# Gathering tokens for a pair of experts with the model's dimension along the free axis, and padding the skipped branches of 32 experts

## The chip, the core and the metric

The kernel runs on one core of a Trainium2 chip, in one launch. The core has five engines, each with an instruction stream of its own: PE (matrix products; weight loads are shown as PEld), DVE and ACT (element work), POOL, and SP, which here issues nearly all DMAs. The metric is the device time of one execution in microseconds, here the median of three runs: 1147.12 us (1146.0 to 1147.28).

## The reference

One layer of a trunk for 256 tokens of 1024 numbers, in float32: a block of three mixers (a short convolution and two kinds of attention) and a layer of 32 experts, of which each token uses four. What matters here is the second half:

```python
logits = (xt @ router_w + router_b)
top_vals, top_idx = lax.top_k(logits, TOP_K)              # TOP_K = 4
top_w = jax.nn.softmax(top_vals, axis=-1)
combine = jnp.einsum('tk,tke->et', top_w, jax.nn.one_hot(top_idx, N_EXPERTS))
def expert_step(acc, params):
    w1, b1, w2, b2, gate_e = params
    u = xt @ w1 + b1
    glu = jnp.minimum(u[:, ::2], SWIGLU_LIMIT)
    lin = jnp.clip(u[:, 1::2], -SWIGLU_LIMIT, SWIGLU_LIMIT)
    a = glu * jax.nn.sigmoid(SWIGLU_ALPHA * glu) * (lin + 1)
    out = a @ w2 + b2
    return acc + gate_e[:, None] * out, None
```

`w1` has 1024x2048 and `w2` 1024x1024 numbers for each expert, 12 MB together.

## The kernel before

About the first 183 us are the mixers, the second norm and the router. Then come 32 experts in a fixed order (the loop over `e`, line 1056). Each reads its weights as twelve tiles of 1 MB, `we{e}_0` to `we{e}_11`, over SP's queue. Twenty tiles are held in a ring of buffers of four kinds (`RING`, line 34); a load is issued by `prefetch` (line 849, the DMA is line 858) when the buffer's last reader is done.

An expert works on 64 slots (`CAP`), the first 64 tokens that chose it. Per pair of experts, `Prepare` (line 759) makes a one-hot matrix `oh` of tokens by 2 x 64 slots, and gathers with products of the normed tokens `xn2` and `oh` into `xg`, which stands with the model's dimension on the partitions; `modulated2` (line 740) scales and shifts it by ACT and DVE. This is done in the middle of the odd expert before the pair; the first pair is gathered earlier, with `half` called piecewise at line 828, before the experts begin.

For each expert PE does the up products `u` in two halves (`first`, line 876), turns the result (`aT`), and does the down products `o` (`second`, line 906). DVE weighs `o` (line 1088), and after each second expert `scatter` adds the pair's `y` to the tokens (line 937). Every product and every turn goes through `mm` or `turn`, so PE's rows all bear lines 83 and 86; tiles tell them apart. A product in float32 shows as two MATMUL rows in the trace and two weight loads.

Where an expert has more than 64 tokens, `if_more` (line 1020) runs before the expert's main path: up to four further blocks of slots, each behind a branch on the count (line 1021). With these inputs that happens for experts 5 and 16, each time with the first block alone (32 more slots). For all others PE jumps over about 1600 instructions. The count is read from memory in `tokens` (line 1047), and `hint` (line 803) puts a branch hint at the start of each main path. `behind_branch` (line 1027) keeps the main path's products behind the branch. The order within one engine is made by a scheduler from the order of the code and the dependencies.

Of the kernel before, what the change touches and what calls it, by code (L numbers as in the profile page):

```python
# [18 lines left out]
P = 128  # L19
# [3 lines left out]
NT = S // P  # L23
# [9 lines left out]
KINDS = {"l": 7, "h": 8, "x": 2, "c": 3}  # L33
RING = "lhhllccchlhhhxhhlllx"
CAP = 64
MORE = ((64, 32), (96, 64), (160, 64), (224, 32))


# [5 lines left out]
def bcast(ap, n):  # L44

    return ap.rearrange("p (a o) -> p a o", o=1).to_broadcast([ap.shape[0], ap.shape[1], n])
# [3 lines left out]
def trunk(ctx: ExitStack, tc: tile.TileContext, x_d, p1_d, p2_d, be_d, ada_d, win_d, wout_d, w1_d, w2_d, out_d):  # L50
    nc = tc.nc
# [10 lines left out]
    def t2k(name, dtype=F32):  # L62
        return tmp.tile([P, 512], dtype, tag="t2", name=name)
# [7 lines left out]
    def pa(name):  # L71
        return psA.tile([P, 2, 512], F32, tag="A", name=name)
# [4 lines left out]
    def pb(name):  # L77
        return psB.tile([P, 512], F32, tag="B", name=name)
# [3 lines left out]
    def mm(out, lhsT, rhs, start, stop):  # L82
        last[:] = [nc.tensor.matmul(out, lhsT, rhs, start=start, stop=stop, skip_group_check=True).ins]  # L83

    def turn(out, in_):
        last[:] = [nc.tensor.transpose(out, in_, ident).ins]  # L86
# [37 lines left out]
    ident = const.tile([P, P], F32, name="ident")  # L124
# [36 lines left out]
    SEL6 = SELE[:, 0:6]  # L161
    slots = const.tile([P, CAP + 32], F32, name="slots")
    iote = const.tile([P, NE], F32, name="iote")
# [25 lines left out]
    for name in order.split():  # L189
        kind, c = name[0], int(name[1:])  # L190
# [66 lines left out]
    xn2 = const.tile([P, NT, D], F32, name="xn2")  # L257
# [440 lines left out]
    def gates(t):  # L698

        nc.scalar.activation(ex[t], lg[t], AF.Exp, bias=rs[t][:, 0:1])  # L700
        nc.vector.scalar_tensor_tensor(weight[:, t, :], ex[t], 1.0, mask[t], op0=ALU.mult, op1=ALU.mult,
                                       accum_out=rs[t][:, 1:2])
        nc.vector.reciprocal(rs[t][:, 2:3], rs[t][:, 1:2])
        nc.vector.tensor_scalar(weight[:, t, :], weight[:, t, :], rs[t][:, 2:3], None, op0=ALU.mult)
# [14 lines left out]
    pos = const.tile([P, NT, NE], F32, name="pos")  # L719
# [9 lines left out]
    def onehot(oh, base, m, es, pos):  # L729

        at = slots[:, base:base + m].rearrange("p (o c) -> p o c", o=1).to_broadcast([P, len(es), m])
        nc.vector.tensor_tensor(oh, at, bcast(pos[:, es[0]:es[0] + len(es)], m), op=ALU.is_equal)

    def gather(ps, oh, t, w, ks=range(KD)):

        for k in ks:
            mm(ps[k * w // 512][:, k * w % 512:k * w % 512 + w], xn2[:, t, k * P:(k + 1) * P], oh.rearrange("p e c -> p (e c)"),
               t == 0 and k * w % 512 == 0, t == NT - 1)

    def modulated2(xg, ps, w):  # L740
        for k in (0, 4, 1, 5, 2, 6, 3, 7):
            o = xg[:, k].rearrange("p e c -> p (e c)")
            x = ps[k * w // 512][:, k * w % 512:k * w % 512 + w]
            if k > 3:
                nc.vector.tensor_scalar(o, x, s2[:, k:k + 1], t2[:, k:k + 1],  # L745
                                        op0=ALU.mult, op1=ALU.add)
            else:
                nc.scalar.activation(o, x, AF.Identity, scale=s2[:, k:k + 1], bias=t2[:, k:k + 1])  # L748

    def slots_first(sc, og, name):  # L750

        ps = pb(f"og{name}")
        for t in range(NT):
            turn(ps[:, t * P:(t + 1) * P], og[:, t].rearrange("p e c -> p (e c)"))
        nc.scalar.copy(sc, ps[:, 0:S])
# [3 lines left out]
    class Prepare:  # L759


        def __init__(self, e):
            self.e = e
            self.oh = sm.tile([P, NT, 2, CAP], F32, tag="part", name=f"oh{e}")
            if e:
# [5 lines left out]
        def half(self, t, ks=range(KD)):  # L771
            if 0 in ks:
                onehot(self.oh[:, t], 0, CAP, [self.e, self.e + 1], pos[:, t])
            gather(self.ps, self.oh[:, t], t, 2 * CAP, ks)

        def rest(self):
            e = self.e
            xg = sm.tile([P, KD, 2, CAP], F32, tag="xg", bufs=1, name=f"xg{e}")
            modulated2(xg, self.ps, 2 * CAP)
            og = sm.tile([P, NT, 2, CAP], F32, tag="part", name=f"og{e}")  # L780
            ox = sm.tile([P, NT, 2, 32], F32, tag="ox", name=f"ox{e}")
            sc = sm.tile([P, S], F32, tag="sc", name=f"sc{e}")
            for t in range(NT):
                if e == 0:
                    gates(t)
                onehot(ox[:, t], CAP, 32, [e, e + 1], pos[:, t])
                nc.vector.tensor_tensor(og[:, t], self.oh[:, t], bcast(weight[:, t, e:e + 2], CAP), op=ALU.mult)
            slots_first(sc, og, e)
            pick = sm.tile([P, 2, P], F32, tag="pick", name=f"pick{e}")
            for i in range(2):  # L790
                nc.gpsimd.tensor_copy(pick[:, i].rearrange("p (q m) -> p q m", q=2).bitcast(F32R),
                                      sel2[:, :, e + i:e + i + 1].to_broadcast([P, 2, CAP]))
            rows[e // 2] = pick
            for i in range(2):
                ready[e + i] = xg[:, :, i, :], sc, ox[:, :, i, :]

    def prepare(e):
        p = Prepare(e)
        for t in range(NT):
            p.half(t)  # L800
        p.rest()

    def hint(e):
# [215 lines left out]

    def if_more(n_e, e, a, aT, blocks=MORE):  # L1020
        with tc.If(n_e > blocks[0][0], label=f"few{e}") if blocks is MORE else tc.If(n_e > blocks[0][0]):  # L1021
            more(e, a, aT, *blocks[0])
            if blocks[1:]:
                if_more(n_e, e, a, aT, blocks[1:])

    @contextmanager
    def behind_branch():
# [19 lines left out]
    def tokens(e):  # L1047

        traced = nc.cur_bb.bb.instructions
        n = len(traced)  # L1050
        value = nc.values_load(cnt[0:1, e:e + 1], min_val=0, max_val=S)
        return value, next(i for i in traced[n:] if i.engine == mybir.EngineType.PE)

    late = None
    n_next, _ = tokens(0)
    for e in range(NE):
        if e:
            prefetch(4)
        xg, sc, _ = ready[e]
        aT = [t1k(f"aT{e}_{G}").rearrange("p (j s) -> p j s", j=2) for G in range(2)]  # L1060
        n_e = n_next
        if_more(n_e, e, t1k(f"am{e}", "partp"), t1k(f"aTm{e}"))
        with behind_branch():
            if e + 1 < NE:
# [12 lines left out]
        if e % 2 and e + 1 < NE:  # L1077
            prepare(e + 1)
# [13 lines left out]
    o, sc, _ = late  # L1092
# [72 lines left out]
```

## Time and profile before

| | |
|---|---|
| median of three runs | 1147.12 us (1146.0 to 1147.28) |
| the profiled execution | 1146.89 us |
| its span, first to last instruction | 1144.9 us |
| PE matmul busy | 1069.5 us (93%) |
| DVE, ACT busy | 389.2 us (34%), 178.6 us (16%) |
| read from HBM | 446.63 MB |
| mean DMA rate | 393 GB/s |
| mean granted PE clock | 0.985 |

PE's matmuls are pipelined and their ends are modelled, so 93% is not PE at its peak. Times below are microseconds from the span's start. An engine's name with a q (SPq, PEldq) is that engine's queue or sequencer: what it issues or waits for beside its work. A stretch's line in the table of windows gives each engine's busy time with its count of instructions, then PE's granted clock (1.00 is full), the busy share of the DMA engines and their rate. "A <- B: t, n, m" in the waits says that A waited t us for B in all, n times, m us at most.

### The profile page before, as it was taken

Reading aid. Unit: us, or ns where it says so; the run is one execution under the profiler, and the core shown is the slowest. Engines: PE = TensorE matmul, PEld = TensorE weight load, DVE = VectorE, ACT = ScalarE, POOL = GpSimd, SP = SyncE. Lnnn points to the kernel's source line nnn. Section 1 sums busy time; section 2 is a strip of 40 time slices with the busy share of each in tenths; the row PEclk is TensorE's granted clock in tenths of the full one; section 3 lists DMA queues with packets and bytes.
Section 4 is the critical chain, followed back from the end, with each engine's and each line's share of the span. In section 5 each row is a group of like instructions: output and inputs, shape, how many; then the busy total and the mean of one; then the engine's idle time right before and its main releaser. Section 6 shows DMA issues by size and latency. Waiting matters only on the chain. (4 is left out here: it accounts for less than half of the span.)

```text
span 1144.9 us, 14101 instructions
## 1 busy us (share of the span) xinstructions
PE 1069.5 (93%) x5432; PEld 467.1 (41%) x5432; DVE 389.2 (34%) x879; ACT 178.6 (16%) x412; POOL 14.5 (1%) x52
## 2 busy tenths in 40 slices
PE   2999999999989999999999989999999999898987
PEld 2887844343333333433333433434343434242322
DVE  7799933222232223222222222232232322231222
ACT  3458622010101010101010100101010101010100
POOL 1000000000000000000000000000000000000000
PEclk7899999999999999999999989999999999999999
DMA  9888899999987999999999999999999999999992
GB/s 383 360 297 311 331 409 370 416 418 417 418 353 309 417 418 417 418 418 417 417 418 416 419 399 404 419 418 418 417 417 419 417 418 417 411 416 410 416 413 110
DMA packets 62913, 449.54 MB, mean 393 GB/s; under 512 B 6960, under 2 KB 7472, under 8 KB 8624
## 3 DMA queue, kind: packets, MB, share of 16 engines
q1 hardware_dynamic: 62336, 447.11, 95.6%
q8 instruction: 79, 1.29, 0.5%
q10 hardware_dynamic: 432, 0.59, 0.1%
q14 instruction: 66, 0.54, 0.1%
HBM read 446.63 MB, written 1.05 MB: 391 GB/s over the span
## 5 line engine op out<-in xcount | busy, mean ns | idle before, releaser
L83 PE MATMUL u<-we,xg 128*64 128x512 f32 (+1 forms) x2304 | 494.2, 577 | 12.7 <-DMA we<-in_w 11.3
L83 PEld LDWEIGHTS u<-we,xg 128*64 128x64 f32 (+1 forms) x2304 | 154.0, 134 | 299.9 <-issue 260.4
L83 PE MATMUL o<-we,aT 128*64 128x512 f32 x1024 | 236.5, 598 | 3.7 <-DMA we<-in_w 3.3
L891 DVE TENSOR_SCALAR sw<-u 128x256 f32<-128x256 f32 (+1 forms) x68 | 28.3, 417 | 441.6 <-PE u L83 429.5
L892 ACT ACTIVATE sw<-sw 128x256 f32<-128x256 f32 (+1 forms) x68 | 27.9, 411 | 666.8 <-DVE sw L891 666.8
L83 PEld LDWEIGHTS o<-we,aT 128*64 128x64 f32 x1024 | 69.6, 136 | 133.2 <-issue 121.8
L1088 DVE TENSOR_TENSOR o<-o,g 64x512 f32<-64x512 f32 x64 | 44.1, 689 | 162.2 <-PE o L83 161.7
L83 PE MATMUL y<-o,sc 128*128 128x512 f32 (+1 forms) x160 | 67.1, 592 | 2.1 <-DVE o L1010 1.3
L83 PEld LDWEIGHTS xg<-oh,xn 128*128 128x128 f32 x512 | 58.6, 192 | 12.6 <-issue 12.4
L83 PE MATMUL xg<-oh,xn 128*128 128x128 f32 x512 | 62.1, 279 | 0.1
L236 DVE SCALAR_TENSOR_TENSOR a<-a,silurow 128x1024 f32<-128x1024 f32 x48 | 57.2, 1216 | 0.0
L745 DVE TENSOR_SCALAR xg<-xg,mods 128x128 f32<-128x128 f32 x64 | 26.0, 410 | 62.7 <-ACT xg L748 61.5
L83 PE MATMUL u<-b,pick 128*128 128x512 f32 x64 | 31.0, 484 | 17.3 <-PEq L1021 16.7
L83 PEld LDWEIGHTS y<-o,sc 128*128 128x128 f32 (+1 forms) x160 | 26.5, 197 | 41.8 <-issue 33.4
L944 DVE TENSOR_TENSOR xr<-xr,y 128x1024 f32<-128x1024 f32 x30 | 36.6, 1221 | 11.8 <-PE y L83 10.4
L904 ACT COPY aT<-aT 128x256 f32<-128x256 f32 x64 | 23.8, 372 | 106.1 <-PE aT L86 106.0
L748 ACT ACTIVATE xg<-xg,mods 128x128 f32<-128x128 f32 x64 | 28.9, 457 | 56.4 <-PE xg L83 45.9
L83 PEld LDWEIGHTS u<-b,pick 128*128 128x128 f32 x64 | 12.1, 189 | 57.1 <-issue 55.9
L86 PEld LDWEIGHTS aT<-ident,a 128*128 128x128 f32 x128 | 14.2, 141 | 50.7 <-issue 33.9
L895 DVE TENSOR_TENSOR a<-a,sw 128x256 f32<-128x256 f32 x64 | 27.4, 428 | 6.8 <-ACT sw L892 0.3
L86 PE MATMUL aT<-ident,a 128*128 128x128 f32 x128 | 27.2, 294 | 2.0
L83 PE MATMUL op<-o,yT 128*128 128x512 f32 x64 | 29.0, 600 | 0.0
(299 smaller groups left out, 750.3 us busy)
## 6 DMA issues: line engine op xcount, KB each, us to landing
we<-in_w SPq DMA_DIRECT2D x383, 1024.0 KB, 19.9
a<-in_ada SPq DMA_DIRECT2D x24, 1024.0 KB, 7.0
w<-in_win SPq DMA_DIRECT2D x12, 1024.0 KB, 11.0
o<-in_wout SPq DMA_DIRECT2D x4, 1024.0 KB, 5.8
xr<-in_x SPq DMA_DIRECT2D x1, 1024.0 KB, 5.3
we<-in_w SPq DMA_DIRECT2D x2, 512.0 KB, 18.1
b1in<-in_be SPq DMA_DIRECT2D x1, 512.0 KB, 5.3
out<-xr SPq DMA_DIRECT2D x2, 256.0 KB, 2.0
```

Source lines behind the costliest of these rows:

```text
L83: last[:] = [nc.tensor.matmul(out, lhsT, rhs, start=start, stop=stop, skip_group_check=True).ins]
L86: last[:] = [nc.tensor.transpose(out, in_, ident).ins]
L236: nc.vector.scalar_tensor_tensor(w[:, i], w[:, i], 1.0, silu_row, op0=ALU.mult, op1=ALU.mult, accum_out=mods[:, m, k:k + 1])
L745: nc.vector.tensor_scalar(o, x, s2[:, k:k + 1], t2[:, k:k + 1], op0=ALU.mult, op1=ALU.add)
L748: nc.scalar.activation(o, x, AF.Identity, scale=s2[:, k:k + 1], bias=t2[:, k:k + 1])
L891: nc.vector.tensor_scalar(gl, u[:, 0:n], 7.0, None, op0=ALU.min)
L892: nc.scalar.activation(sg, gl, AF.Sigmoid, scale=1.702)
L895: nc.vector.tensor_mul(ln, ln, sg)
L904: nc.scalar.copy(aT.rearrange("p j s -> p (j s)"), ps[:, 0:n])
L944: nc.vector.tensor_add(xr[:, t, :], xr[:, t, :], y.rearrange("p h m -> p (h m)"))
L1088: nc.vector.tensor_mul(o[64 * (e % 2):64 * (e % 2) + 64, 512 * h:512 * h + 512], ps[r, :], g2[r, :])
```

## The change

`Prepare` gets a second way to gather, `beside`, and `prepare` calls it for all pairs but the first. It multiplies the other way round: the one-hot matrix is the weight and 512 columns of the tokens run through, so that the result `xs` has slots on the partitions and the model's dimension along. Four products replace sixteen. ACT copies the two halves out of PSUM, and eight turns of 128x128 put them into `xg` as before.

In the innermost branch of `if_more` (taken only by an expert with more than 224 tokens) `FILL[e]` turns of the identity are added, whose result nobody reads. They lengthen PE's stream between the branch and the main path.

```diff
+FILL = (99, 1, 93, 100, 107, 116, 107, 115, 107, 116, 107, 115, 107, 116, 107, 115, 107, 116, 107, 115, 107, 116, 107, 115, 107, 116, 107, 115, 107, 116, 107, 0)
...
+        def beside(self):
+
+            at = pa(f"xs{self.e}")
+            for t in range(NT):
+                onehot(self.oh[:, t], 0, CAP, [self.e, self.e + 1], pos[:, t])
+            for h in range(2):
+                for t in range(NT):
+                    mm(at[:, h, :], self.oh[:, t].rearrange("p e c -> p (e c)"), xn2[:, t, h * 512:h * 512 + 512], t == 0, t == NT - 1)
+            for h in range(2):
+                xs = t2k(f"xs{self.e}_{h}")
+                nc.scalar.copy(xs, at[:, h, :])
+                for k in range(4):
+                    turn(self.ps[h][:, k * P:(k + 1) * P], xs[:, k * P:(k + 1) * P])
+
...
     def prepare(e):
         p = Prepare(e)
-        for t in range(NT):
-            p.half(t)
+        p.beside()
         p.rest()
...
             if blocks[1:]:
                 if_more(n_e, e, a, aT, blocks[1:])
+            elif FILL[e]:
+                fill = pb(f"fill{e}")
+                for _ in range(FILL[e]):
+                    turn(fill[:, 0:P], ident)
```

PE in expert 7, where the pair of experts 8 and 9 is gathered, before (u7 and o7 are the up and down products, og8 the gates' turn; a last x4 is four rows alike):

```order
L83 MATMUL u7_1_7393<-we7_7_6064,xg6_6000 64x512 x4
L83 MATMUL xg8_7433<-oh8_7432,xn2_246 128x128 x16
L86 MATMUL og8_7468<-ident_80,og8_7461 128x128 x2
L1051 TENSOR_LOAD cnt_1525
L83 MATMUL o7_7475<-we7_8_6744,aT7_0_6779 64x512 x4
L86 MATMUL aT7_1_7480<-ident_80,a7_1_7412 128x128 x2
```

The same place with the change, where lines 83 and 86 have become 86 and 89:

```order
L86 MATMUL u7_1_8142<-we7_7_6593,xg6_6525 64x512 x4
L86 MATMUL xs8_8183<-xn2_246,oh8_8181 128x512 x4
L89 MATMUL og8_8218<-ident_80,og8_8211 128x128 x2
L1071 TENSOR_LOAD cnt_1525
L86 MATMUL o7_8225<-we7_8_7377,aT7_0_7412 64x512
L89 MATMUL xg8_8182<-ident_80,xs8_0_8190 128x128 x4
L89 MATMUL xg8_8182<-ident_80,xs8_1_8196 128x128 x4
L86 MATMUL o7_8225<-we7_8_7377,aT7_0_7412 64x512 x3
L89 MATMUL aT7_1_8230<-ident_80,a7_1_8161 128x128 x2
```

Four products and eight turns stand for the sixteen products; the gates' turn and one product of `o` have come between the products and the turns.

PE at the start of expert 0's main path, before (y0_224 is the last product of the fourth block that is jumped over, u0_0 the first up products of the path):

```order
L83 MATMUL y0_224_01_2260<-o0_224_2251,sc0_224_2104 128x256 x2
L83 MATMUL y0_224_10_2264<-o0_224_2251,sc0_224_2104 128x256 x2
L83 MATMUL y0_224_11_2268<-o0_224_2251,sc0_224_2104 128x256 x2
L1021 UNCONDITIONAL_BRANCH x5
L1161 BRANCH_PREFETCH_HINT
L83 MATMUL u0_0_2273<-b1_222,pick0_1630 128x512
L83 MATMUL u0_0_2273<-we0_0_1633,xg0_1602 64x512 x4
```

With the change:

```order
L86 MATMUL y0_224_01_2260<-o0_224_2251,sc0_224_2104 128x256 x2
L86 MATMUL y0_224_10_2264<-o0_224_2251,sc0_224_2104 128x256 x2
L86 MATMUL y0_224_11_2268<-o0_224_2251,sc0_224_2104 128x256 x2
L89 MATMUL fill0_2272<-ident_80 128x128 x87
L1037 UNCONDITIONAL_BRANCH x5
L1181 BRANCH_PREFETCH_HINT
L86 MATMUL u0_0_2373<-b1_222,pick0_1630 128x512
L86 MATMUL u0_0_2373<-we0_0_1633,xg0_1602 64x512 x4
```

The path itself is the same. The fill's turns (87 here and 12 among the rows ahead of these, each a weight load and a matmul) have moved it by 198 places, and with it the branch on expert 1's count at the path's end, which the scheduler puts ahead of the last seven products of `o`. In the later experts the paths with a gather also have 32 instructions fewer.

## Rows read from the trace of the kernel before

**Rows 1.** From the page: of the 40 slices (28.6 us each) the DMA engines' busy share and the rate.

```profile
DMA  9888899999987999999999999999999999999992
GB/s 383 360 297 311 331 409 370 416 418 417 418 353 309 417 418 417 418 418 417 417 418 416 419 399 404 419 418 418 417 417 419 417 418 417 411 416 410 416 413 110
```

**Rows 2.** The table of windows: stretch, its length, PE, PEld, DVE, ACT and POOL busy with their counts, PE's granted clock, DMA share, GB/s.

```profile
344.60:348.80 4.20, 4.12 (x11) 1.33 (x13) 1.33 (x7) 0.00 (x0) 0.00 (x0) 0.59 0.01 2
348.80:670.00 321.20, 308.74 (x1569) 118.67 (x1565) 82.65 (x187) 30.91 (x79) 3.19 (x12) 1.00 1.01 415
670.00:700.00 30.00, 28.49 (x116) 10.22 (x116) 9.73 (x18) 1.20 (x3) 0.00 (x0) 0.83 0.97 387
700.00:1108.00 408.00, 388.48 (x1757) 143.68 (x1757) 102.86 (x225) 36.61 (x92) 3.19 (x12) 1.00 1.01 416
...
1122.00:1132.00 10.00, 8.63 (x36) 2.23 (x34) 1.60 (x4) 0.79 (x2) 0.00 (x0) 1.00 0.07 28
```

**Rows 3.** SP's own queue: its longest sum of waits from 323 to 350 us, the issue that ended that wait (start, length), and the longest sum from 660 to 700 us.

```profile
SPq L858 <- PE u L83: 24.2, 1, 24.2
...
348.72 0.33 SPq L858 DMA_DIRECT2D we<-in_w  x1
...
SPq L858 <- PE u L83: 22.8, 9, 8.8
```

**Rows 4.** The chain of work that ended last, in order of time (start, length, what): the links near the end.

```profile
1001.44 20.86 DMA we<-in_w
...
1022.39 19.91 DMA we<-in_w
...
1112.57 19.88 DMA we<-in_w
...
1132.58 3.67 PE o L83 x16
```

**Rows 5.** The table of windows for the first and the fifth of the stretches from one expert's start to the next, and what PE waited for from 348 to 700 us (of weights).

```profile
182.70:210.30 27.60, 27.22 (x112) 9.02 (x112) 5.65 (x19) 4.18 (x9) 1.48 (x2) 1.00 0.97 383
...
296.90:323.00 26.10, 25.97 (x111) 8.88 (x111) 6.67 (x12) 1.58 (x4) 0.00 (x0) 1.00 1.02 418
...
PE o L83 <- DMA we<-in_w: 3.1, 3, 1.3
```

**Rows 6.** PE in order of time (start, length, operation, shapes, count): the eight turns of h2ps and the products behind them; the gather in expert 5 with the next two rows; the scatter in expert 6 with the row behind it.

```profile
162.33 1.04 PE L86 MATMUL h2ps<-ident,xr 128*128 128x128 f32 x8
163.28 1.98 PE L83 MATMUL op<-o,yT 128*128 128x512 f32 x4
...
362.57 3.84 PE L83 MATMUL xg<-oh,xn 128*128 128x128 f32 x32
366.25 0.38 PE L86 MATMUL og<-ident,og 128*128 128x128 f32 x2
366.56 1.94 PE L83 MATMUL o<-we,aT 128*64 128x512 f32 x8
...
381.99 3.70 PE L83 MATMUL y<-o,sc 128*128 128x512 f32 x8
385.52 0.38 PE L86 MATMUL aT<-ident,a 128*128 128x128 f32 x2
```

**Rows 7.** ACT: copies of 128x512 out of PSUM (count, ns least, median, most), and the sigmoid beside the gather of rows 6.

```profile
L661 ACT COPY h2T<-h2ps x2: 585/585/585, 163.0 to 173.2; 128x512 f32<-128x512 f32 x2
...
363.14 0.42 ACT L892 ACTIVATE sw<-sw 128x256 f32<-128x256 f32 x1 [6.24 <-DVE sw L891]
```

**Rows 8.** PE's own branches on the counts (count, ns least, median and most, first and last start us): all of them, and one each behind experts 0, 3, 9, 10, 16 and 29.

```profile
L1021 PEldq COMPARE_BRANCH  x36: 74/348/6017, 181.2 to 1104.2; - x36
...
L1021 PEldq COMPARE_BRANCH  x1: 430/430/430, 204.3 to 204.3; - x1
...
L1021 PEldq COMPARE_BRANCH  x1: 3181/3181/3181, 292.1 to 292.1; - x1
...
L1021 PEldq COMPARE_BRANCH  x1: 6017/6017/6017, 479.4 to 479.4; - x1
...
L1021 PEldq COMPARE_BRANCH  x1: 5092/5092/5092, 507.5 to 507.5; - x1
...
L1021 PEldq COMPARE_BRANCH  x1: 5982/5982/5982, 701.7 to 701.7; - x1
...
L1021 PEldq COMPARE_BRANCH  x1: 3722/3722/3722, 1073.2 to 1073.2; - x1
```

**Rows 9.** PE's first work behind a branch (start, length, what, count, idle time before it and what ended it): behind expert 0, behind expert 5, and behind experts 9 and 10.

```profile
206.78 3.64 PE L83 MATMUL o<-we,aT 128*64 128x512 f32 x14 [0.28 <-PEq L1021]
...
374.57 0.47 PE L83 MATMUL u<-b,pick 128*128 128x512 f32 x1 [0.41 <-PEq L1021]
...
485.82 0.47 PE L83 MATMUL u<-b,pick 128*128 128x512 f32 x1 [1.99 <-PEq L1021]
...
513.05 0.47 PE L83 MATMUL u<-b,pick 128*128 128x512 f32 x1 [1.06 <-PEq L1021]
```

**Rows 10.** PE's first 32 up products of expert 5, behind its extra rows, and of expert 6.

```profile
345.08 8.75 PE L83 MATMUL u<-we,xg 128*64 128x512 f32 x32
...
374.97 7.09 PE L83 MATMUL u<-we,xg 128*64 128x512 f32 x32
```

**Rows 11.** From the page's DMA queues: the larger kind of instruction transfers (count, MB, share of 16 engines).

```profile
q8 instruction: 79, 1.29, 0.5%
```

## The prediction

> **What bounds the kernel now.** I began with the page's slices. From the sixth on the core reads about 417 GB/s nearly throughout, with two dips [rows 1], so the expert stage is a stream of weights and the question is where the stream stops. Windows answer that [rows 2]: between 344.60 and 348.80 us the DMA share is 0.01, from 348.80 to 670 it is 1.01, from 670 to 700 it is 0.97, from 700 to 1108 again 1.01. The waits of SP's own queue say why it stops at 345: one issue, at 348.72, waited 24.2 us for PE's products [rows 3], longer than the 20 us that a load takes from issue to landing at full stream [rows 4], so the queue ran dry. In 660 to 700 the longest wait for PE was 8.8 us [rows 3], and the queue still held work.
>
> The last window is the strangest. From 1122 to 1132 us the share is 0.07 and the rate 28 GB/s [rows 2]: 0.07 of sixteen DMA engines is about one engine. So one engine finishes some 11 us after the others, and the chain of waits hangs on it: links of 19.9 and 20.8 us, each a load from issue to landing, up to 1132.44, then only the last products and the store [rows 4]. A link of eight loads takes about 19.9 us, and most have 0.9 us on top. This engine was given work without a pause from the restart at 348.7 on, so I take the end to be the restart plus a fixed amount. Then only what moves the restart moves the time.
>
> The restart is PE's doing. In the five stretches from 182.70 to 323.00 PE is busy nearly all the time (27.22 of 27.60 us in the first, 25.97 of 26.10 in the last) [rows 5]; it is the clock of that stage, up to the extra rows of expert 5, whose main path begins at 344.7. After 348.8 PE runs against a stream that is slower than itself (from 348 to 700 it waits 3.1 us for weights in all [rows 5]) and its time is slack, as long as SP's waits stay under about 20 us.
>
> **The change part by part.** *The gather.* A pair's gather is now 32 PE rows from 362.57 to 366.25, that is 3.68 us [rows 6]. It becomes four products of 128x512 and eight turns. Four such products in fp32 with a 128x128 weight are the scatter's eight rows, 381.99 to 385.52: 3.53 us. Eight turns of 128x128 took 0.95 us from 162.33 to 163.28 [rows 6]. So a pair costs 3.53 + 0.95 - 3.68 = 0.8 us more. The turns wait for two ACT copies of 128x512, 0.585 us each [rows 7]. The first copy runs under the second pair of products (1.77 us). The second has the two turns of og (366.25 to 366.56, 0.31 us), one product of o and the first four turns over it, together about 1.0 us against 0.585 and a semaphore way of some 0.1 at either end; I cost it at nothing, and at 0.6 us a pair if that cover is gone. ACT is free at that point (its sigmoid ends at 363.56) [rows 7]. The modulation behind the turns gets xg about 1.5 us later, and has some 4 us before the next path begins; hidden. Before the restart two pairs are gathered this way (for experts 2 and 4; that of experts 0 and 1 is unchanged): +1.6 us, between +1.2 and +2.8.
>
> *The placing.* The fill products stand in the innermost branch, which does not run here; they only move addresses. What an address does is seen in the durations of PE's own branches. The median of 36 is 0.35 us, and a few take up to 6.0 [rows 8]. I counted the places in PE's compiled stream, label marks left out, and took each branch's place in a block of 256: 187 took 5.98 us, 188 took 6.02, 203 took 5.09, 204 took 3.18, 220 took 3.72. The four from 235 to 252 took 0.35 to 2.06, those at 1 to 172 at most 0.5. [...] Four microseconds of that are covered, since PE's sequencer runs ahead of its array: a path usually begins with a gap of 0.41 us, and behind two of the three longest waits with 1.99 and 1.06 [rows 9].
>
> Counted so, the new paths do not begin at one place. With label marks in the count they do (place 3 or 4 each time), but there are nine marks for each expert, and the durations above fall in line only without them; then the start falls from 250 (expert 0) by 8 to 10 per expert. So the branches behind experts 6 to 29 come to lie at harmless places or under cover; the losses at 485 and 513 go, but they lie behind the restart and are slack. Before the restart the placing hurts once. The branch behind expert 0, at place 1 before, comes to 198, between 188 and 204. There the cover is thin: it starts at 204.3, and PE's array has work only to 206.5 [rows 8, 9]. A branch of d us lets PE go on at about 204.3 + d + 0.4: with d = 3.18 that is 1.1 us late, with 5.09 it is 3.0, with 6.02 it is 3.9. I take 4.6 (nearer to the neighbour at 203) and so +2.5 us, with 0 and +3.9 as ends. The branch behind expert 3 comes to 214; with 3 to 5 us it stays under its 4.6 us of cover, at worst +0.6. That behind expert 4 (188) falls through, which took 0.08 us before.
>
> *The clock.* [...] Expert 5's first 32 products took 8.75 us instead of 7.09 [rows 10]. As nearly all products before the restart were slow, a shift can only give up to 1.8 us back. I take none.
>
> *Elsewhere.* At 670 to 700 PE would be later against the stream by five more pairs, 4 us, less 2.2 for the two long gaps gone. A wait of 8.8 + 2 us is still under 20, so the last engine does not pause. The tail behind 1132.44 has no changed line.
>
> Sum: +1.6 + 2.5 = +4.1 us. The profiled execution took 1146.89 us (span 1144.9 and 2.0 around it), 0.23 under the median of 1147.12. 1146.89 + 4.1 = **1151.0 us**.
>
> **The rivals.** *Only the gather counts.* The target may come in time behind expert 0: before, place 204 waited 2 us less than place 203, so the place alone does not settle it. Then +1.6: 1148.5.
>
> [...]
>
> *Not slower: the engine that ends last has less to read.* Its 0.9 us on top of a link comes about once for each expert (25 between the restart and the end, 24 us). If these were PE's instruction reads (79 of 16 KB on the page [rows 11], about two for each expert), paths within one block could halve them, -12 us: 1151 - 12 = 1139. Against it: they come once and PE's reads twice. From five fewer of them on the kernel is no longer slower.
>
> *The waits go as named.* If paths did begin on a block, the gaps of 0.28 to 0.41 us before the restart (four) could go, -1.4, against +1.6 for the gather: 1147.1.
>
> *Worse.* The second copy uncovered (+0.6 a pair), the full wait behind expert 0 (+3.9), and 0.6 behind expert 3: 1.6 + 1.2 + 3.9 + 0.6 = +7.3, 1154.
>
> **How the numbers follow.** The forecast (1149.5 to 1152.5) 0.48, only the gather 0.26, waits gone 0.08, worse 0.12, fewer reads 0.06. A measurement of this kernel tells about 0.2%, 2.3 us, from no change, so slower begins at 1149.4: the forecast nearly whole, worse, and a little of the second (0.04) make 0.63; faster is the fewer reads and a lucky clock, 0.07; the rest 0.30 is the same. The range of 8 in 10 leaves out the fewer reads and half of the worse case: 1147.0 to 1153.6.
>
> **What would show it.** The branch near 204 us takes 3 to 6 us, and the 14 products of o behind it begin at 208 to 210 rather than 206.78. Products of xs take 3.5 us and turns 0.95, without a gap between. Expert 5's extra rows and the long wait of SP end about 4 us later, at 352.8 rather than 348.7, and from there to the last landing it is again 783.7 us. A chain with fewer links of 20.8, a DMA share that is 1.01 through 344 to 349, or a landing time that does not follow the restart would prove me wrong.

## The result and the profile after

The changed kernel takes 1160.71 us (median of 5; 1157.70 to 1161.41) against 1147.28 us of the kernel before in the same session: ratio 1.0108, 95% interval 1.0091 to 1.0126. So it is slower, as forecast, but by 13.4 us where 4.1 were forecast, and outside the range of 1147.0 to 1153.6. The profiled execution took 1160.65 us (span 1158.6), 13.76 more than that of before.

The page's slices of the changed kernel (29.0 us each), the DMA engines' busy share and the rate, answer to [rows 1]:

```profile
DMA  9888899999996999999999997999999999999993
GB/s 382 354 304 318 338 390 385 362 406 382 417 392 240 380 418 419 418 418 417 418 418 418 417 403 298 418 417 418 417 419 417 417 417 418 418 418 417 419 417 158
```

The dip at slice 13 is deeper (240 instead of 309), the slice behind it has one too (380), and slice 25 (695 to 724 us) fell to 298; before, the dip there was 399 at its lowest. The windows show the same places in the columns of [rows 2]:

```profile
206.20:210.70 4.50, 0.00 (x0) 0.00 (x0) 0.11 (x1) 0.00 (x0) 0.00 (x0) 1.00 1.01 410
210.70:214.30 3.60, 3.56 (x10) 1.21 (x12) 1.08 (x6) 0.00 (x0) 0.00 (x0) 0.53 0.59 241
...
354.20:358.40 4.20, 4.20 (x13) 1.27 (x15) 1.19 (x6) 0.00 (x0) 0.00 (x0) 0.59 0.01 2
...
400.00:690.00 290.00, 282.24 (x1340) 99.19 (x1336) 75.19 (x173) 31.81 (x78) 2.66 (x10) 1.00 1.01 418
690.00:712.00 22.00, 15.88 (x54) 5.56 (x54) 5.60 (x9) 0.79 (x2) 0.00 (x0) 0.77 0.68 267
712.00:1121.00 409.00, 402.36 (x1668) 138.00 (x1666) 102.67 (x226) 44.44 (x107) 3.19 (x12) 1.00 1.01 416
```

From 206.20 to 210.70 PE does nothing at all, and in the 3.6 us behind that its granted clock is 0.53. The dry queue before expert 5's main path is the same as before, only later. From 690 to 712 the DMA engines are busy for 0.68 of the time: a second dry queue, which before did not have.

PE's own branches behind experts 0 and 5, expert 16's inner one, and the one behind expert 30 (columns as in [rows 8]):

```profile
L1037 PEldq COMPARE_BRANCH  x1: 6732/6732/6732, 203.7 to 203.7; - x1
...
L1037 PEldq COMPARE_BRANCH  x1: 5537/5537/5537, 381.0 to 381.0; - x1
...
L1037 PEldq COMPARE_BRANCH  x1: 5977/5977/5977, 690.2 to 690.2; - x1
...
L1037 PEldq COMPARE_BRANCH  x1: 345/345/345, 1118.1 to 1118.1; - x1
```

Behind expert 0, PE in order of time; then the gather of a pair at 430 us, which answers to [rows 6]:

```profile
203.12 2.79 PE L86 MATMUL o<-we,aT 128*64 128x512 f32 x10
210.74 5.34 PE L86 MATMUL o<-we,aT 128*64 128x512 f32 x14 [4.83 <-PEq L1037]
...
429.80 3.70 PE L86 MATMUL xs<-xn,oh 128*128 128x512 f32 x8
433.33 0.38 PE L89 MATMUL og<-ident,og 128*128 128x128 f32 x2
433.64 1.07 PE L86 MATMUL o<-we,aT 128*64 128x512 f32 x2
434.65 1.09 PE L89 MATMUL xg<-ident,xs 128*128 128x128 f32 x8
435.67 1.93 PE L86 MATMUL o<-we,aT 128*64 128x512 f32 x6
437.54 0.44 PE L89 MATMUL aT<-ident,a 128*128 128x128 f32 x2
```

Against [rows 9] the 14 rows of o start at 210.74 instead of 206.78 and take 5.34 instead of 3.64 us. In the gather the turns stand inside o's products. Eight rows of o took 1.94 us before [rows 6]; here two take 1.07 us by themselves and the other six 1.93 more. An o product is written in two column halves (two rows each). Where the halves stood one behind the other, the trace has two rows under way at once (from 366.60 to 366.90 us before, and again from 435.72 to 436.05 here), and a couple took 0.94 us (eight rows in 1.87, from 366.56 to 368.43). The turns part one such couple; its first half ran with no row beside it (from 433.70 to 434.00) and took 1.01 us, from 433.64 to 434.65, and the six rows behind the turns took as long as eight in a row, 1.87 us from 435.67 to 437.54: 1.0 us lost for each pair of experts.

ACT's copies of the same pair:

```profile
433.59 1.07 ACT L789 COPY xs<-xs 128x512 f32<-128x512 f32 x2 [2.81 <-PE xs L86]
```

Both copies begin behind the last product (PE's next rows, og's turns, begin at 433.33, the copies at 433.59). The first does not run under the second half of the products.

SP's own queue, the longest waits for PE around 358 us, at 380 and from 660 to 730 us (sum, count, longest):

```profile
SPq L874 <- PE u L86: 26.5, 2, 25.2
...
SPq L874 <- PE o L86: 7.3, 1, 7.3
...
SPq L874 <- PE u L86: 32.8, 9, 17.5
```

The first answers to the 24.2 us of [rows 3] and ends at 358.15 instead of 348.72. The last was 8.8 us before. The chain of work that ended last looks as in [rows 4]:

```profile
1125.31 20.86 DMA we<-in_w
...
1146.30 3.67 PE o L86 x16
```

The end is still set by one DMA engine that lags: from 1140 to 1146 us the DMA engines' busy share is 0.06 to 0.08, about one of sixteen. From SP's restart to the last products it is 1146.30 - 358.15 = 788.15 us, before 1132.58 - 348.72 = 783.86. So of 13.7 us, 9.4 arose ahead of the restart and 4.3 behind it. The trace also has the landing of each load. Counted from the restart and set against before, the lagging engine's landings lose 1.6 us up to the 20th load and 2.7 more from 700 to 730 us, and nothing elsewhere.

### The profile page after: what moved, and what is told of

Its sections match the earlier page's. It is cut to its first block, busy times and chain, and to the rows that moved or that the text cites. A ratio compares the mean times of both kernels' runs of the same rounds, so it can differ in the third digit from the quotient of the medians.

```text
span 1158.6 us, 13666 instructions
## 1 busy us (share of the span) xinstructions
PE 1092.1 (94%) x5192; PEld 450.4 (39%) x5192; DVE 389.1 (34%) x879; ACT 194.5 (17%) x442; POOL 14.4 (1%) x52
## 5 line engine op out<-in xcount | busy, mean ns | idle before, releaser
L86 PE MATMUL o<-we,aT 128*64 128x512 f32 x1024 | 253.1, 602 | 6.2 <-PEq L1037 4.8
L86 PEld LDWEIGHTS o<-we,aT 128*64 128x64 f32 x1024 | 72.9, 137 | 138.2 <-issue 135.5
L86 PE MATMUL xs<-xn,oh 128*128 128x512 f32 x120 | 55.5, 605 | 0.0
L86 PEld LDWEIGHTS xs<-xn,oh 128*128 128x128 f32 x120 | 21.6, 190 | 33.7 <-issue 33.7
```

## The experiments

All kernels were compared with the kernel before, run in the same session (medians of 1146.85 to 1147.60 us). The diffs are against the changed kernel, but the last one. Since FILL stands in code that does not run, other numbers in it move addresses and nothing else. "Place" is the count of the prediction: PE's compiled instructions without label marks, modulo 256; that 256 is the right number no run shows.

**Gather and placing apart.** First gather_only:

```diff
-FILL = (99, 1, 93, 100, 107, 116, 107, 115, 107, 116, 107, 115, 107, 116, 107, 115, 107, 116, 107, 115, 107, 116, 107, 115, 107, 116, 107, 115, 107, 116, 107, 0)
+FILL = (0, 16, 0, 16, 127, 16, 0, 16, 127, 16, 0, 16, 127, 16, 0, 16, 127, 16, 0, 16, 127, 16, 0, 16, 127, 16, 0, 16, 127, 16, 0, 0)
```

> The new gather, with the numbers of FILL chosen so that each expert's branch stands where it stood before the change (places 1, 93, 142, 205, 219, ... modulo 256, at most one off). Theory (the loss is the gather's o split, 1.88 us a pair, plus branches that wait by where they stand, plus a second dry queue at expert 16): no wait of more than 0.5 us behind expert 0, no low clock behind it, SP's long wait ends near 348.7 + 3.8 = 352.5 us, the inner branch of expert 16 takes about 0.33 us, and the time is +3.8 us on before (up to +5.5 if SP's wait at 660 to 730 grows beyond 18 us). Rival 1 (the gather alone is the whole loss): +12 to +14. Rival 2 (the gather costs 0.8 us a pair as predicted, the rest is placing): +1.6.

For places_only, the gather of before and other numbers:

```diff
-        p.beside()
+        for t in range(NT):
+            p.half(t)
...
+FILL = (99, 113, 93, 84, 108, 100, 107, 99, 108, 100, 107, 99, 108, 100, 107, 99, 108, 100, 107, 99, 108, 100, 107, 99, 108, 100, 107, 99, 108, 100, 107, 0)
```

> The gather of before, with the numbers of FILL chosen so that each expert's branch stands where the change put it (places 198, 4, 238, 213, 188, 197, ... modulo 256, at most one off). Theory: the branch behind expert 0 takes 6 to 7 us, the low clock follows it, and SP's long wait ends near 348.7 + 5.7 = 354.4 us; expert 16's inner branch waits about 6 us as in the change, but the queue there has 3.8 us and more in hand without the slower gathers, so of the second dry queue at most 2 us stay: +5.7 to +7.7 us. Rival 1 (the gather alone): 0. Rival 2 (the gather as predicted, the rest placing): +12.

Measured: gather_only 1156.70 us, ratio 1.0086 [1.0069, 1.0103]; places_only 1157.67 us, 1.0110 [1.0078, 1.0143]. Neither expectation held, and the two sum to 20.7, more than the change's 13.4. Their traces tell why. In gather_only the branch behind expert 3, at 205 instead of 204 but at the end of a path that is 32 instructions shorter, took 6.04 us instead of 3.18 and left PE a gap of 2.01 us; taking that away (gather_clear, below) took 3.4 us off, 1.5 of them in the trace at that branch. In places_only the wait behind expert 0 came as expected (6.19 us, a gap of 4.29, then 14 rows of o in 6.30 us), but it also had a wait of 6.16 us at the last branch, 1112.84 us, with a gap of 4.56 in the tail, and its inner branch of expert 16 took 0.33 us. So each brought waits of its own, and the place alone does not tell the wait. The branch behind expert 1 shows it best: it stands at place 4 in the change and in e0_moved (below), at the end of the same path, and took 1.56 us in the one (at 241.3 us) and 0.34 in the other (at 236.3).

**The branch behind expert 0, and the one in expert 16's block.**

```diff
+FILL = (0, 100, 93, 100, 107, 116, 107, 115, 107, 116, 107, 115, 107, 116, 107, 115, 107, 116, 107, 115, 107, 116, 107, 115, 107, 116, 107, 115, 107, 116, 107, 0)
```

> The change, with FILL[0] 0 and FILL[1] 100 instead of 99 and 1: expert 0's path and the branch behind it stand where they stood before (1 instead of 198), all others as in the change. Theory: the branch behind expert 0 takes 0.43 us instead of 6.73, no low clock behind it, SP's long wait ends near 358.2 - 5.7 = 352.5 us, and with the dry queue at expert 16 still there the time is 5 to 6 us under the change's. Rival (the wait would come up again at the next late branch, or the stream's end does not follow the restart): within 2 us of the change.

```diff
+FILL = (99, 1, 93, 100, 107, 116, 107, 115, 107, 116, 107, 115, 107, 116, 107, 115, 117, 106, 107, 115, 107, 116, 107, 115, 107, 116, 107, 115, 107, 116, 107, 0)
```

> The change, with FILL[16] 117 and FILL[17] 106 instead of 107 and 116: the end of expert 16's branch and its main path lie 20 instructions later, all others as in the change. [...] Rival 1 (the wait comes from where that branch itself stands, or from the length of the block's code): it stays near 6 us and the time is the change's. Rival 2 (the wait goes but the pause at 702 to 710 us comes from elsewhere): 0.33 us and the same time.

> The two edits of e0_moved and e16_moved together, in the change. Theory: expert 16's inner branch takes 0.33 us instead of 5.9, its dry queue (2 to 2.6 us in the trace of e0_moved, between the landings at 693 and 745 us) goes, and the time is 1.7 to 2.6 us under that of e0_moved (1155.5): about 1153.3, that of gather_clear. Rival (as e16_moved alone suggests, whose time was the change's): that of e0_moved within 0.7 us.

Measured: e0_moved 1155.46 us, 1.0074 [1.0057, 1.0091], 5.3 us under the change by the medians, as the theory said. Its branch behind expert 0:

```profile
L1037 PEldq COMPARE_BRANCH  x1: 425/425/425, 204.9 to 204.9; - x1
```

e16_moved was expected to take the inner branch's wait away, and 3.5 to 4.5 us off the change's time with it. The inner branch fell,

```profile
L1037 PEldq COMPARE_BRANCH  x1: 328/328/328, 691.8 to 691.8; - x1
```

but the time is 1160.18 us, 1.0105 [1.0083, 1.0127]: not told apart from the change. In its trace the landings of the lagging engine no longer lose time at 700 to 730 us, but 1.4 us more were lost at 360 to 420 (3.0 instead of 1.6). With expert 0's wait out of the way the gain shows: e0_e16_moved took 1153.64 us, 1.0055 [1.0042, 1.0068], 1.8 us under e0_moved. SP's longest wait for PE from 660 to 730 us, of e0_moved and then of e0_e16_moved:

```profile
SPq L874 <- PE u L86: 36.1, 12, 16.6
```

```profile
SPq L874 <- PE u L86: 35.9, 16, 10.8
```

In the 22 us from 685 us on (684 in e0_e16_moved) the DMA engines are busy for 0.67 of the time in e0_moved, and for 0.92 in e0_e16_moved. So the wait of the inner branch is a matter of 20 instructions, and the second dry queue is its work; the intervals of the two times overlap, so the 1.8 us rest on the traces too (e0_moved's landings lose 2.0 us there, those of e0_e16_moved 0.1). Why 20 instructions decide it, no trace shows.

**How many pairs count.** gather_clear moves the branch behind expert 3 off its bad place (`FILL[3]` and `FILL[4]` 56 and 87 instead of 16 and 127); then the old gather is put back for the first pairs, as shown in gather_from_6, and with `e < 8` in gather_from_8. The first numbers of `FILL`, not shown, follow so that the branches stay where gather_clear has them:

```diff
-        p.beside()
+        if e < 6:
+            for t in range(NT):
+                p.half(t)
+        else:
+            p.beside()
```

> As gather_only, but with FILL[3] 56 and FILL[4] 87 instead of 16 and 127, which moves the branch behind expert 3 from place 205, where it took 6.04 us and left PE a gap of 2.01, to 29: no branch before expert 10's waits any more, the gather is the new one. Theory (1.88 us for each of the two pairs before the restart, and 1.5 to 3 us lost behind it, since a pair now holds SP for 7.3 us until o's products while few loads are queued): from expert 0's branch to the end of SP's long wait 167.5 + 3.8 = 171.3 us (gather_only had 173.5), the time +5 to +7 us on before. Rival (behind the restart nothing is lost by the gather): the same 171.3 us, the time +3.8.

> The new gather for the pairs of experts 6 on, the old one for experts 2 and 4; branches where gather_clear has them. Theory (the pair that expert 5's path gathers for expert 6 counts too, because only one load is queued when SP waits for it, some 20 us behind the restart): SP's long wait ends as in before (167.5 us from expert 0's branch), the issue after it waits 7.7 us instead of 5.9 with one load left in the queue, and the time is +1.7 to +2.3 us on before. Rival (only what is ahead of the restart counts): within 0.5 us of before.

> As gather_from_6, with the old gather for expert 6 too. Theory: from expert 8 on the queue holds three or more loads and the gather is hidden: within 0.6 us of before. Rival (each pair adds to the time, or the thin queue lasts longer): +1 us or more.

Measured: gather_clear 1153.30 us, 1.0057 [1.0043, 1.0071]; gather_from_6 1149.59 us, 1.0023 [1.0013, 1.0033]; gather_from_8 1147.30 us, 1.0001 [0.9988, 1.0013]. That is as the theory had it (gather_from_6 just above its 2.3). The pair that expert 5's path gathers, behind the restart, costs 2.3 us by the medians. SP's wait some 20 us behind the restart, in gather_from_6 and then in gather_from_8:

```profile
SPq L878 <- PE o L86: 7.3, 1, 7.3
```

```profile
SPq L878 <- PE aT L89: 5.8, 1, 5.8
```

At that moment one or two loads are under way (before: issues at 362.67 and then 368.54 us, landings at 372.44 and 376.12). Later, waits of 7.3 us did no harm (gather_from_8 has them too from 400 us on, and took 1147.30 us); here one costs time. From expert 8 on three and more loads are queued (three were under way in the change when SP went on at 437.63 us, behind the gather of 429.80), and the slower gather is hidden. The landings of all the kernels agree: up to the 60th load behind the restart they lose 1.1 to 3.0 us against before in the ten kernels that gather the third pair the new way, and 0.1 to 0.6 us in the three that gather it the old way (places_only, gather_from_8 and bias_later, below).

**What a pair's cost is made of.** In o_whole the order is fixed by hand, so that o is not parted:

```diff
+        queue(lambda: p.turns(0),
+              p.gates_turned,
+              lambda: p.turns(1))
...
-        with tc.issue_after(read):
+        with tc.issue_after(last[0] if e % 2 and e + 1 < NE else read):
```

Here gates_turned is the part of rest that makes og and sc.

> As gather_clear, but the order on PE is fixed: the products of xs, four turns, the two turns of og, four turns, and only then o's products, so that no turn stands between the two column halves of one o product. Theory (the split of o costs 1.0 us of a pair's 1.88, and makes SP's wait on o 7.3 us): a pair costs 0.8 to 0.9 us, from expert 0's branch to the end of SP's long wait 167.5 + 1.7 = 169.2 us, SP's longest wait on o under 6 us, at most 0.5 us lost behind the restart, the time +1.7 to +2.2 us on before. Rival 1 (the cost is in the products or turns themselves): 171 us and the time of gather_clear. Rival 2 (the loss behind the restart has nothing to do with the wait on o): 169.2 us, and the time +3.2 to +4.7.

(`FILL` again follows; not shown.) It took 1153.41 us, 1.0051 [1.0038, 1.0065]: no gain. PE's rows of a pair:

```profile
227.62 3.70 PE L86 MATMUL xs<-xn,oh 128*128 128x512 f32 x8
232.05 0.66 PE L89 MATMUL xg<-ident,xs 128*128 128x128 f32 x4 [0.73 <-ACT xs L789]
232.54 0.38 PE L89 MATMUL og<-ident,og 128*128 128x128 f32 x2
232.76 0.60 PE L89 MATMUL xg<-ident,xs 128*128 128x128 f32 x4
233.29 1.94 PE L86 MATMUL o<-we,aT 128*64 128x512 f32 x8
235.16 0.44 PE L89 MATMUL aT<-ident,a 128*128 128x128 f32 x2
```

o's eight rows are whole again (233.29 to 235.16, 1.87 us), but now PE stands 0.73 us for ACT's copy. The split had been the cover for the copy: most of the cost only changed its name. A pair costs 1.7 us in this trace (117.71 - 114.33 = 3.38 us for two, between the branches of the table below), not the 1.95 that the next expectation gives it. That figure holds 0.58 us of another kind: my edit had also moved a copy of ACT in front of two modulations of expert 0, and from the branch ahead of expert 0 to the one behind it took 23.65 us instead of 23.07. Next, the halves of xs went into two PSUM tiles:

```diff
-            at = pa(f"xs{self.e}")
+            at = [pb(f"xs{self.e}_{h}") for h in range(2)]
```

> As o_whole, but the two halves of xs lie in two PSUM tiles instead of one, so that ACT's first copy waits for the first four trace rows of the products only and runs under the last four. In o_whole both copies began behind the last product (231.41 us), PE stood 0.73 us for the first, and a pair still cost 1.95 us. Theory (the pair costs what its rows cost once the copies are covered and o is kept whole): no idle of PE ahead of the turns, a pair costs 3.53 + 0.95 - 3.68 = 0.8 to 0.9 us, three pairs (those for experts 2, 4 and 6) count, the time is +2.2 to +3.0 us on before. Rival (the turns or the products themselves are slower beside the copies): a pair stays at 1.5 us or more, +4.5 and more.

> As two_tiles, but the pair of experts 0 and 1, which this study did not mean to touch, again has ACT's copy of sc behind its four modulations instead of between them (that had put 0.58 us into expert 0's start). In the trace of two_tiles a pair cost 1.0 us, from the branch of expert 1 to that of expert 5 (116.4 us against 114.3 of before and 118.2 of gather_clear), and the pair behind the restart 1.0. Theory (three pairs count, 1.0 us each): 116.4 us between those branches and +2.6 to +3.6 us on before. Rival (something else in that order costs the rest of the 5.9 us that two_tiles lost): the time stays over +4.5.

two_tiles took 1153.17 us, 1.0055 [1.0042, 1.0068], two_tiles_e0 1151.73 us, 1.0033 [1.0021, 1.0046]. In the first that copy of ACT still stood in front of the two modulations, and expert 0's stretch took 24.74 us, with a clock of 0.81 and 0.86 at 176 to 186 us beside it; in two_tiles_e0 it took 23.08. PE's rows of a pair in two_tiles_e0, and ACT's first copy:

```profile
226.87 3.70 PE L86 MATMUL xs<-xn,oh 128*128 128x512 f32 x8
230.41 0.60 PE L89 MATMUL xg<-ident,xc 128*128 128x128 f32 x4
230.84 0.38 PE L89 MATMUL og<-ident,og 128*128 128x128 f32 x2
231.25 0.66 PE L89 MATMUL xg<-ident,xc 128*128 128x128 f32 x4
231.83 1.94 PE L86 MATMUL o<-we,aT 128*64 128x512 f32 x8
...
228.94 0.59 ACT L789 COPY xc<-xs 128x512 f32<-128x512 f32 x1 [1.09 <-PE xs L86]
```

The first copy now begins at 228.94, under the second half of the products, no wait of PE is left, and from the gather's begin to o's it is 231.83 - 226.87 = 4.96 us instead of 366.56 - 362.57 = 3.99 [rows 6]: a pair costs 1.0 us, near the predicted 0.8. The total, +4.1, is above the expected 2.6 to 3.6, though. In its profiled execution expert 5's extra rows took 0.86 us longer, and 2.2 us were lost behind the restart where 1.0 was expected. The landings lose them within the first sixteen loads, so they belong to the thin queue; why they are 2.2 there, and 1.1 in two_tiles with the same rows of a pair, is not settled.

**A kernel that beats both.** If PE's work ahead of the restart sets the time, work moved behind it is gained. Against the kernel before (with FILL for the places):

```diff
-            scatter(*late, e == 2)
+            scatter(*late, e == 10)
```

> The kernel before with its own gather, and the products of the second biases (b2 with the gates, 8 of them) moved from expert 2's path, ahead of the restart, to expert 10's, behind it; FILL keeps the branches of experts 1, 2 and 5 on where they stood and takes that behind expert 3 off its place near a block's end. If the time is PE's work up to expert 5's extra rows plus a fixed stream, expert 2's path falls from 30.1 us to the 26.6 of expert 4's, SP's long wait ends 3.5 us earlier than in before counted from expert 0's branch (164.0 instead of 167.5), and the time is 3.0 to 3.6 us under before: 1143.4. Rival (the end does not follow the restart, because another engine of the DMA or the trunk sets it): within 1 us of before.

It took 1143.18 us, ratio 0.9967 [0.9955, 0.9978]: 4.0 us under the kernel before, a little more than expected, and 17.5 under the changed one. The chain's last products, which answer to 1132.58 in [rows 4]:

```profile
1129.60 3.67 PE o L86 x16
```

The traces of the kernels side by side, in us: from the branch on expert 1's count (the one behind expert 0) to that on expert 5's, where SP's long wait ended, and from there to the last products of o.

| kernel | branch 1 to 5 | restart at | restart to last o |
|---|---|---|---|
| before | 114.33 | 348.72 | 783.86 |
| the change | 124.34 | 358.15 | 788.15 |
| e16_moved | 124.53 | 359.03 | 786.73 |
| e0_moved | 118.10 | 352.75 | 788.90 |
| e0_e16_moved | 118.07 | 353.05 | 786.35 |
| gather_clear | 118.16 | 352.96 | 786.05 |
| gather_from_6 | 114.33 | 348.58 | 787.68 |
| gather_from_8 | 114.32 | 350.51 | 784.73 |
| bias_later | 110.84 | 345.34 | 784.26 |

Two pairs cost 118.10 - 114.33 = 3.8 us, 1.9 each. The wait behind expert 0, with the granted clock of 0.53 behind it, costs 124.34 - 118.10 = 6.2. The second biases are worth 3.5. A single execution's last column strays by a microsecond or so (gather_from_8's restart is also late by chance, 0.9 us in expert 0's start and 0.9 in expert 5's extra rows), so what lies behind the restart is read from the medians and the landings.

## Why the prediction was right and wrong

By medians the 13.4 us are: two pairs of the gather ahead of the restart and a third behind it, 6.1 (gather_clear); expert 0's branch, 5.3 (3.9 by the ratios, 6.2 in the traces); expert 16's inner branch, 1.8 (0.5 when it alone was removed). The branch behind expert 5 cost nothing that shows: in places_only it took 5.67 us and left PE a gap of 1.65, and the landings lost 0.4 us up to the 60th load. (That e0_e16_moved has it, gather_clear does not, and they differ by 0.3 does not settle it, since gather_clear's branches behind experts 10 and 16 take 6.05 and 6.15 us instead of 0.33 and 0.35.)

In the terms of the prediction's sum, read from the traces: two pairs cost 3.8 us where +1.6 stood, and the branch behind expert 0 cost 4.5 where +2.5 stood. Three terms had been put at nothing: the clock behind that branch (1.7), the third pair (2.3 by the medians) and expert 16's inner branch (1.8 by the medians, 2.7 by the change's landings).

- **The direction, and where it would be decided: right.** PE ahead of the restart sets the end; bias_later gained its 3.5 us there nearly one for one.
- **"A pair costs 0.8 us": wrong, 1.9.** The products took 3.53 us and the turns 1.02, nearly as summed; that alone makes 0.9. Two steps failed. The first copy was thought to run under the second two products; with both halves in one PSUM tile it began behind the last (433.59 us, some 0.1 behind the products' modelled end at 433.50). And the "two turns of og, one product of o" that I counted as its cover were not free: that one product stood without the column half that runs beside it, and that cost 1.0 us. The cover of "about 1.0 us", less 0.31 for og's turns and some 0.5 for four turns of xg, leaves some 0.2 for that product; alone it took 1.01. With o kept whole the copy had no cover (o_whole, 0.73 us of waiting); with two tiles and o whole a pair cost 1.0.
- **"Before the restart two pairs are gathered this way": the term that was left out.** A third pair, gathered 10 to 20 us behind the restart, counts as well, 2.3 us. "As long as SP's waits stay under about 20 us" was read at full stream; with one load left a wait of 7.3 us was enough.
- **The branch behind expert 0: right in kind, too small.** It waited 6.73 us, longer than any before and above the upper end of 6.02. The step "PE goes on at 204.3 + d + 0.4" held: 203.71 + 6.73 + 0.4 is 210.84, and PE began at 210.74. That is 7.03 us behind the branch's start instead of 2.49, 4.5 us late, where I took 2.5.
- **"The clock: I take none": wrong by 1.7 us.** Only the gain at 345 us was weighed. The stop of 4.5 us at 206 was followed by a granted clock of 0.53 from 210.70 to 214.30 us, and the next 14 rows took 5.34 us instead of 3.64.
- **"At 670 to 700 a wait of 8.8 + 2 us is still under 20": wrong.** It became 17.5, with 20.0 us from one issue to the next (681.40 to 701.40), and the lagging engine did pause. Only the branches from one main path to the next had been counted, not the inner one that an expert with extra rows takes. In e0_moved and e0_e16_moved the last column of the table differs by 2.6 us for it.
- **The places: half right.** Those behind experts 0, 3 and 5 (198, 214, 197) waited 6.73, 2.88 and 5.54 us, near the 3.18 to 6.02 us of places 187 to 220 before, and the gaps at 485 and 513 went. But behind expert 30 place 211 took 0.35 us, and in two_tiles_e0 places 171 and 155, harmless before, took 6.2 and 6.1:

```profile
L1047 PEldq COMPARE_BRANCH  x1: 6232/6232/6232, 877.8 to 877.8; - x1
...
L1047 PEldq COMPARE_BRANCH  x1: 6117/6117/6117, 1048.6 to 1048.6; - x1
```

So what 36 durations showed by place does not carry over to other layouts. That from expert 7 on no path's branch waits in the change (0.36 us at most) fits the count with label marks; that either count, or its 256, decides a wait was my reading, and no run shows it.

Of the rivals, "only the gather" (+1.6) falls with e0_moved (the branch behind expert 0 takes 6.73 us in the change, 0.43 there), "fewer reads" with the links of 20.86 us that are still there, and "the waits go as named" with the branch behind expert 0. "Worse" (+7.3) was nearest; of its parts the full wait behind expert 0 came, the others did not.

## What to carry to other kernels

Ask of a queue how many transfers it holds at the moment of a wait, not only how long the wait is: behind the restart it held one or two here, and a pair gathered there cost 2.3 us, while the same gather later cost nothing. Where products are written in column halves, keep the halves next to each other in the order (here 0.94 us for two, 1.01 for one alone); and a cover is priced with what it costs to be moved there. Where code addresses decide waits (20 instructions took one from 5.98 to 0.33 us here), change them in the dead code and look at every branch, the inner ones too, rather than trust a counted rule.

## What the runs showed of the hardware

PE's branches on the counts took from 0.07 to 6.73 us in the changed kernel, and 20 instructions more ahead of one's target made the difference in two pairs of kernels (5.98 us in the change and 0.33 in e16_moved; 5.92 in e0_moved and 0.33 in e0_e16_moved). In the changed kernel PE stood for 4.83 us before 210.74; from 210.70 to 214.30 us its granted clock was 0.53, and the next 14 rows of o took 5.34 us instead of 3.64. Behind stops of 3.99 us in e16_moved and 4.29 in places_only they took 6.36 and 6.30. In these programs two parts of one PSUM tile were released together to ACT, at the last product (its copies began at 433.59 us in the change, with the products from 429.80 to 433.33, and at 231.41 in o_whole); in two tiles the first copy ran under the second half's products (it began at 228.94 us in two_tiles_e0, with the products from 226.87 to 230.41; PE did not wait, against 0.73 us in o_whole). Two column halves of 64 ran beside one another as neighbours, and one that was parted from its neighbour ran alone: 1.01 us for one alone (433.64 to 434.65 in the change), 1.87 / 4 = 0.47 us each in an unbroken row of four.
